# Attention with bias on one core: k and q of pair 2 ahead of V of pair 0, and a wait for the sixth load ahead in the prologue

## Chip, core and metric

The kernel runs on one core of a Trainium2 chip. The metric is device time in microseconds of one execution; the kernel before was run three times. The core's engines work side by side and meet through semaphores: TensorE (PE: matrix products and transposes, with weight loads listed apart as PEld), VectorE (DVE), ScalarE (ACT), GpSimd (POOL), and SyncE (SP), which only issues DMA transfers. PE, ACT and DVE each execute their instructions in the order in which the program lists them, and so do the queues that issue transfers.

## What is computed

Four batches of eight heads, each with 1024 positions and 64 dimensions; one bias of 1024 x 1024 for all heads.

```
scores = scale * matmul(q, k.T) + bias          # scale = 1/8
attn   = exp(scores - max) / sum(exp(scores - max))
out    = matmul(attn, v)                        # f32, (4, 8, 1024, 64)
```

## The kernel before

**Tiling.** The 32 heads are taken in 16 pairs, because two heads of 64 dimensions fill the 128 partitions. A head's 1024 queries are cut into 8 chunks of 128. One unit of work, a *slot* (256 in all), is one chunk of one head: eight products of 128 x 128 write the scores of 128 queries against 1024 keys into one of three places in PSUM (`pl0` to `pl2`, line 87; the fill is at L244), an exponential on ACT reads the place and writes the tile E (L258), and later eight products of E with V give the output with the row sums beside it (L312). DVE takes the reciprocal and scales (L320, L322), and SP stores. 19 slots, listed in `PLAN`, have their exponential computed on DVE instead (L275 to L295).

**Bias once for many heads.** Scores stay in their PSUM place from one head to the next: the bias of a chunk is put in once by products (L241), and each later head adds the difference from the head before. That is why a pair has `ko` and `qo` for its odd head and `ke` and `qe` for the even one, which hold rows of this pair and of the pair ahead of it. L199 and L201 copy `ko` and `qo` out of PSUM; L210 and L212 make the doubles in `ke` and `qe`; for later pairs, and for half of `ke` from pair 2 on, SP copies by DMA (L539).

**Loads.** k, q and V arrive in f32 and are turned to bf16 by the transfer itself, which POOL issues: L145 for k, L155 for q, L165 for V, L160 for a bias chunk. k and q of a pair are transposed on PE (L191) into PSUM tiles `px` that share two PSUM tiles with the output banks `po`; V is copied by DVE into `vall` (L493), which the products of L312 read. There are three landing tiles for V (`VL`), five each for k and q (`LANDS`). A transfer issued on POOL has one of eight semaphores in turn and waits for the transfer that had it before, so at most eight of POOL's loads are out at a time.

**What sets the order.** The first instructions stand by hand (lines 337 to 392): the loads of pair 0, then bias chunks 1 and 2, k of pair 1, the first part of q of pair 1, V of pair 0, k of pair 2 and q of pair 2 on POOL. From line 394 a planner writes the rest of the program: it keeps a clock for each engine (`t_pe`, `t_act`, `t_dve`, `t_pool`, `t_sp`), asks for each possible next step when it could start by estimated costs and landing times, and records the step that is first. `raw_at` holds the time at which k or q of a pair is taken to have landed, `vland_at` that of V; `t_dma` is the clock of the load queue. These are estimates that decide the order alone; on the chip semaphores decide.

`early` issues the 21 loads of the list in line 772: k3, q3, V1, k4, q4, V2, k5, q5, V3, k6, q6, V4, V5, bias 3, the rest of q0, bias 4, V6, the rest of q1, bias 5, 6 and 7. All later loads (pair 7 on) come from `load` and `next_v`. Both go through `issue`, whose third argument is a depth: where it is above 0, POOL first copies one element of the load that stands so many places back in `flight` into `tick` (L468), which can only run once that load has landed.

```
if 0 < depth <= len(flight):
    what, t = flight[-depth]
    nc.gpsimd.tensor_copy(tick[:], what)
    at = max(at, t + 100)
```

`load` and `next_v` use a depth of 2 or 3 (`LATE`); `early` uses 0.

Of the kernel before, what the change touches and what calls it, by code (L numbers as in the profile page):

```python
# [16 lines left out]
def kernel(  # L17
# [30 lines left out]
    SPLIT, EARLY = 2, 7  # L48
# [84 lines left out]
    def beside(pr, x):  # L133

        raws[pr, x, 0] = t = land.tile([P, 2, NCH, D], BF, name="qk"[x] + "16").rearrange(
            "p t c d -> p (t c d)").rearrange("p (c t d) -> p c t d", t=2, d=D)
        for y in range(2):
            nc.gpsimd.dma_start(out=t[:, :, y, :], in_=(qf, kf)[x][pr][:, y].rearrange("p (c d) -> p c d", d=D))  # L138
        return t[:1, NCH - 1, 1, D - 1:]

    def load_k(pr):
        if pr >= EARLY and 1 in BESIDE:
            return beside(pr, 1)
        lands[pr, 1, 0] = t = land.tile([P, 2, NCH, D], BF, name="k16")
        nc.gpsimd.dma_start(out=t.rearrange("p t c d -> p t (c d)"), in_=kf[pr])  # L145
        return t[:1, 1, NCH - 1, D - 1:]

    def load_q(pr, cs):
        if pr >= EARLY and 0 in BESIDE:
            return beside(pr, 0)  # L150

        t = consts.tile([P, 2, NCH - C0, D], BF, name=f"qrest{pr}") if cs.start else land.tile([P, 2, NCH, D], BF, name="q16")
        lands[pr, 0, cs.start] = t
        to = t[:, :, :cs.stop - cs.start, :]
        nc.gpsimd.dma_start(out=to.rearrange("p t c d -> p t (c d)"),  # L155
                            in_=qf[pr][:, :, cs.start * D:cs.stop * D])
        return to[:1, 1, cs.stop - cs.start - 1, D - 1:]
# [5 lines left out]
    def load_v(pr):  # L163
        lands[pr, "v"] = vland.tile([P, 2, NCH, D], BF, name="v16")
        nc.gpsimd.dma_start(out=lands[pr, "v"].rearrange("p t c d -> p t (c d)"),  # L165
                            in_=vf[pr].rearrange("p t c d -> p t (c d)"))
        return lands[pr, "v"][:1, 1, NCH - 1, D - 1:]
# [167 lines left out]
    with tc.manual_schedule():  # L335
# [17 lines left out]
            load_b(c)  # L353
        load_k(1)
        load_q(1, slice(0, C0))
        load_v(0)
        load_k(2)
        load_q(2, slice(0, NCH))
        for i in range(10):
            nc.tensor.matmul(places[2][:, 0, :], zeros[:, :P], zeros, start=True, stop=True)  # L360

# [35 lines left out]
        ISSUE, COPY = 70, 7000  # L397
        T0 = 8600.0
        bias_at = {0: T0, 1: T0, 2: 9600}
        raw_at = {(1, 1, 0): 10800, (1, 0, 0): 11500, (2, 1, 0): 14300, (2, 0, 0): 16000}  # L400
        v_at, vland_at = {}, {0: 13000}
        t_dma = 15500
        DUE = (62, 84, 100, 38, 118, 109, 123, 147, 135)
        t_pe, t_act, t_dve, t_pool = 9300.0, 9900.0, 9600.0, 9000
# [31 lines left out]
        E1, E2 = 1400, 1700  # L436
        free_lands, loads, loads_v = set(), list(range(EARLY, NP)), []
        sp_q, t_sp = [], T0
        AHEAD, SLACK = 60, 300
# [23 lines left out]
        def issue(at, cost, depth, load, pr, *a):  # L463

            nonlocal t_dma
# [4 lines that stand above are left out]
            at = pool(at, 750)  # L470
            t_dma = max(t_dma + cost, at + 2200 + cost)
            flight.append((load(pr, *a), t_dma + 200))
            return t_dma + 200

        def load(pr, t):
            raw_at[pr, 1, 0] = issue(t, 1600, LATE, load_k, pr) + SLACK
            raw_at[pr, 0, 0] = issue(t, QCOST, LATE, load_q, pr, slice(0, NCH)) + SLACK
            for p in [pr - 1] * (pr > EARLY) + [pr] * (pr + 1 == NP):
                loads_v.append(p)
            next_v(t)  # L480
# [10 lines left out]
        def move_v(pr):  # L491
            def run(t2):
                nc.vector.tensor_copy(vall[:, 2 * pr % VR:2 * pr % VR + 2, :, :D], lands[pr, "v"][:])  # L493
                v_at[pr] = t2 + 480 + L_DVE
                next_v(v_at[pr])
            dve_q.append((vland_at[pr] + VSLACK * (pr >= EARLY), 0.3, 480, run))


        def early(kind, pr):
            if kind == "k":  # L500
                raw_at[pr, 1, 0] = issue(0, E1, 0, load_k, pr) + SLACK
            elif kind == "q":
                cs = slice(0 if pr >= SPLIT else C0, NCH)
                raw_at[pr, 0, cs.start] = issue(0, E1 if pr >= SPLIT else E2, 0, load_q, pr, cs) + SLACK
            elif kind == "v":
                vland_at[pr] = issue(0, E1 if pr < 5 else E2, 0, load_v, pr)
                move_v(pr)
            else:
                bias_at[pr] = issue(0, E2, 0, load_b, pr)

        def doubles(pr, which, c0, n, t2, urgent):
            if not which and pr >= EARLY:
# [165 lines left out]
        def pool(at, cost=0):  # L678
            nonlocal t_pool
            t_pool = max(t_pool, at) + cost  # L680
            return t_pool
# [90 lines left out]
        for x in ("k3", "q3", "v1", "k4", "q4", "v2", "k5", "q5", "v3", "k6", "q6", "v4", "v5", "b3", "q0", "b4", "v6", "q1", "b5", "b6", "b7"):  # L772
            early(x[0], int(x[1]))
# [71 lines left out]
```

## Time and profile before

| | us |
|---|---|
| median of 3 runs | 234.18 (233.77 to 234.87) |
| the profiled execution | 234.37 |
| its span, first to last instruction | 232.6 |
| granted TensorE clock in it | 0.998 of full |

The profile is that of one execution. The span is what its views cover; the execution's own time is 1.8 us longer. A row of the timeline gives the start, the length, the engine, the line of the code, the operation, what it writes from what it reads, how many instructions are taken together, and in brackets how long the engine idled before and what ended that. In the list of exponentials the mean of one (1104 ns) is longer than the step from one to the next, because they overlap in the pipeline. The last number of a DMA issue row is the time from the issue to the landing.

### The profile page before, as it was taken

What the parts mean: (1) busy time and instruction counts of PE and PEld (TensorE: products, weight loads), DVE (VectorE), ACT (ScalarE), POOL (GpSimd) and SP (SyncE); (2) the same over time, 40 slices, a digit from 0 to 9 for tenths busy, and PEclk for the clock granted to TensorE, in tenths of its full rate; (3) what the DMA queues carried; (4) which work ended last, traced back from release to release, by engine and by line L of the source; (5) the groups of instructions that cost most, each with busy time, mean ns of one, the idle gap of its engine ahead of it and who ended that gap; (6) DMA issues with size and microseconds to landing.
All of it is one profiled execution on the core that took longest, in us unless ns stands there. A gap on an engine that the chain in (4) does not pass through costs nothing.

```text
span 232.6 us, 10671 instructions
## 1 busy us (share of the span) xinstructions
PE 223.1 (96%) x4671; PEld 209.8 (90%) x4671; DVE 197.4 (85%) x294; ACT 221.6 (95%) x242; POOL 61.6 (27%) x99
## 2 busy tenths in 40 slices
PE   7979999899999999999999999999999999999993
PEld 2869997899999999999999999999998999999992
DVE  3566777599988998989889789899999899999993
ACT  3799999899999999999999999999999999999994
POOL 8844440155633524445244110000000000000000
PEclk9999999999999999999999999999999999999999
DMA  6999999899999999989899865111112122112212
GB/s 205 205 205 218 222 225 216 188 108 121 152 176 141 153 183 143 135 183 194 150 241 216 188 107 130 43 37 39 42 29 57 34 53 50 58 28 74 70 37 62
DMA packets 55645, 29.75 MB, mean 128 GB/s; under 512 B 31856, under 2 KB 51952, under 8 KB 55600
## 3 DMA queue, kind: packets, MB, share of 16 engines
q0 software_dynamic: 30336, 14.06, 48.5%
q1 hardware_dynamic: 24832, 14.43, 22.5%
q8 instruction: 36, 0.59, 1.0%
q10 hardware_dynamic: 432, 0.59, 0.8%
q14 instruction: 9, 0.07, 0.1%
HBM read 29.36 MB, written 8.39 MB: 162 GB/s over the span
## 4 chain that ended last, share of the span: by engine, by line
PE 42%; ACT 30%; issue 14%; DMA 5%; DVE 4%; POOL 3%; SPq 2%; DVEq 0%; ACTq 0%; POOLq 0%
ACT E L258 30%; PE pl L244 24%; PE po L312 12%; DMA q<-in_q_dram 4%; PE px L191 4%; SPq L694 2%; PE pl L241 2%; DVE ob L322 1%; DMA out_dram<-ob 1%; DVE dy L275 1%; POOL k L145 1%; DVE df L280 1%; POOL braw L160 1%; DVE dt L290 0%; DVE de L295 0%
## 5 line engine op out<-in xcount | busy, mean ns | idle before, releaser
L258 ACT ACTIVATE E<-pl 128x1024 bf16<-128x1024 f32 (+1 forms) x238 | 218.5, 1104 | 3.5 <-PE pl L244 3.1
L312 PE MATMUL po<-vall,E 128*128 128x65 bf16 x1896 | 92.0, 194 | 1.5 <-DVE ob L322 0.8
L312 PEld LDWEIGHTS <-E 128*128 128x128 bf16 x1896 | 77.4, 98 | 2.8 <-ACT E L258 1.1
L244 PE MATMUL pl<-qo,ko 128*128 128x128 bf16 x1024 | 76.8, 219 | 0.8 <-ACT E L258 0.2
L244 PEld LDWEIGHTS <-ko 128*128 128x128 bf16 x1160 | 69.4, 98 | 3.9 <-issue 0.7
L244 PE MATMUL pl<-qe,ke 128*128 128x128 bf16 x888 | 66.3, 219 | 1.7 <-issue 0.6
L244 PEld LDWEIGHTS <-ke 128*128 128x128 bf16 x888 | 53.5, 98 | 4.6 <-issue 0.7
L275 DVE TENSOR_SCALAR dy<-pl 128x1024 int32<-128x1024 f32 x19 | 23.2, 1221 | 4.5 <-PE pl L244 3.7
L322 DVE TENSOR_TENSOR ob<-po,rs 128x448 f32<-128x448 f32 (+2 forms) x40 | 23.2, 581 | 2.7 <-DMA out_dram<-ob 0.8
L284 DVE SCALAR_TENSOR_TENSOR dt<-df 128x1024 f32<-128x1024 f32 x19 | 23.2, 1220 | 0.3
L295 DVE SCALAR_TENSOR_TENSOR de<-dy,dt 128x1024 uint16<-128x1024 int32 x19 | 23.1, 1218 | 0.1
L287 DVE SCALAR_TENSOR_TENSOR df<-dt,df 128x1024 f32<-128x1024 f32 x19 | 23.1, 1218 | 0.1
L290 DVE SCALAR_TENSOR_TENSOR dt<-df,dt 128x1024 f32<-128x1024 f32 x19 | 23.0, 1217 | 0.1
L138 POOL DMA_DIRECT2D q<-in_q_dram x18 | 16.4, 911 | 2.9 <-PE pl L244 1.6
L201 DVE TENSOR_SCALAR qo<-px,sgn 128x1024 bf16<-128x1024 bf16 (+2 forms) x18 | 12.4, 687 | 4.9 <-PE px L191 3.2
L165 POOL DMA_DIRECT2D v<-in_v_dram x16 | 11.6, 728 | 16.3 <-DVE rs L320 7.5
L199 DVE COPY ko<-px 128x1024 bf16<-128x1024 bf16 (+1 forms) x16 | 10.7, 670 | 5.5 <-PE px L191 5.3
L320 DVE RECIPROCAL rs<-po 128x7 f32<-128x7 f32 (+3 forms) x42 | 8.1, 193 | 6.7 <-PE po L312 6.3
L280 DVE TENSOR_SCALAR df<-dy 128x1024 f32<-128x1024 uint16 x19 | 13.0, 686 | 0.1
L241 PE MATMUL pl<-ident,braw 128*128 128x128 bf16 x136 | 11.5, 228 | 0.1
L145 POOL DMA_DIRECT2D k<-in_k_dram x15 | 10.6, 710 | 2.5 <-DMA k<-in_k_dram 0.9
L468 POOL COPY tick<-q 1x1 bf16<-1x1 bf16 x9 | 3.3, 365 | 28.4 <-DMA q<-in_q_dram 28.4
(54 smaller groups left out, 126.2 us busy)
## 6 DMA issues: line engine op xcount, KB each, us to landing
v<-in_v_dram POOLq DMA_DIRECT2D x16, 256.0 KB, 6.6
k<-in_k_dram POOLq DMA_DIRECT2D x15, 256.0 KB, 6.0
out_dram<-ob SPq DMA_DIRECT2D x35, 96.0 KB, 3.9
ke<-ko SPq DMA_DIRECT2D x22, 128.0 KB, 4.4
out_dram<-ob SPq DMA_DIRECT2D x40, 64.0 KB, 2.5
q<-in_q_dram POOLq DMA_DIRECT2D x18, 128.0 KB, 5.2
out_dram<-ob SPq DMA_DIRECT2D x68, 32.0 KB, 2.9
qe<-q SPq DMA_DIRECT2D x17, 128.0 KB, 5.0
```

The lines of the kernel that those rows point to most:

```text
L138: nc.gpsimd.dma_start(out=t[:, :, y, :], in_=(qf, kf)[x][pr][:, y].rearrange("p (c d) -> p c d", d=D))
L241: nc.tensor.matmul(to, braw[:, c, :].rearrange("p (kp kc) -> p kc kp", kc=NCH)[:, kc, :], ident8[:], start=i == 0, stop=False, skip_group_ ...
L244: nc.tensor.matmul(to, kk[:, kc, :], qq[:, c, :], start=False, stop=True, skip_group_check=True)
L258: nc.scalar.activation(e[:, i:i + n].rearrange("p b x -> p (b x)"), places[slots[s][0]][:, i:i + n].rearrange("p b x -> p (b x)"), ACTF.Ex ...
L275: w.tensor_scalar(t["y"][:], places[slots[s][0]].rearrange("p b x -> p (b x)"), scale * LOG2E * 65536.0, 127.0 * 65536.0, op0=ALU.mult, op ...
L280: w.tensor_scalar(t["f"][:], t["lo"], G / 65536.0, None, op0=ALU.mult)
L284: w.scalar_tensor_tensor(t["t"][:], t["f"][:], -G, t["f"][:], op0=ALU.add, op1=ALU.mult)
L287: w.scalar_tensor_tensor(t["f"][:], t["t"][:], Q, t["f"][:], op0=ALU.mult, op1=ALU.add)
L290: w.scalar_tensor_tensor(t["t"][:], t["f"][:], V, t["t"][:], op0=ALU.add, op1=ALU.mult)
L295: w.scalar_tensor_tensor(etile[s].bitcast(U16).rearrange("p c q -> p (c q)"), t["y"][:], 1.0 / 512.0, t["t"][:], op0=ALU.mult, op1=ALU.add)
L312: nc.tensor.matmul(po[:, j + i, :], etile[s][:, kc, :], vall[:, slots[s][2] % VR, kc, :], start=j + i + kc == 0, stop=kc == NCH - 1, skip_ ...
L322: nc.vector.tensor_tensor(ob[:, :n, :], po[:, :n, :D], rs[:, :n, :].to_broadcast([P, n, D]), op=ALU.mult)
```

## The change

Two edits. The first takes V of pair 0 behind k and q of pair 2 in the hand-written list, and gives the planner matching landing times. The second calls `issue` in `early` with a depth of 6 instead of 0.

```
         load_k(1)
         load_q(1, slice(0, C0))
-        load_v(0)
         load_k(2)
         load_q(2, slice(0, NCH))
+        load_v(0)
...
-        raw_at = {(1, 1, 0): 10800, (1, 0, 0): 11500, (2, 1, 0): 14300, (2, 0, 0): 16000}
-        v_at, vland_at = {}, {0: 13000}
+        raw_at = {(1, 1, 0): 10800, (1, 0, 0): 11500, (2, 1, 0): 12700, (2, 0, 0): 14300}
+        v_at, vland_at = {}, {0: 16300}
...
         def early(kind, pr):
             if kind == "k":
-                raw_at[pr, 1, 0] = issue(0, E1, 0, load_k, pr) + SLACK
+                raw_at[pr, 1, 0] = issue(0, E1, 6, load_k, pr) + SLACK
             elif kind == "q":
                 cs = slice(0 if pr >= SPLIT else C0, NCH)
-                raw_at[pr, 0, cs.start] = issue(0, E1 if pr >= SPLIT else E2, 0, load_q, pr, cs) + SLACK
+                raw_at[pr, 0, cs.start] = issue(0, E1 if pr >= SPLIT else E2, 6, load_q, pr, cs) + SLACK
             elif kind == "v":
-                vland_at[pr] = issue(0, E1 if pr < 5 else E2, 0, load_v, pr)
+                vland_at[pr] = issue(0, E1 if pr < 5 else E2, 6, load_v, pr)
                 move_v(pr)
             else:
-                bias_at[pr] = issue(0, E2, 0, load_b, pr)
+                bias_at[pr] = issue(0, E2, 6, load_b, pr)
```

The depth takes hold from the seventh of the 21 loads: k5 waits for k3, q5 for q3, and so on to bias 7, 15 copies (L468) more on POOL. What follows in the program: on PE the transposes of k2 stand ahead of fill 6 instead of behind fill 7, those of q2 ahead of fill 8 instead of behind it, and the first product with V stands behind fill 11 instead of fill 13 (fills are counted as slots, from 0); from fill 19 on, PE's order is that of before. On DVE the copy of V0 moves behind the first double of q2, and the first evacuation of an output bank moves ahead of q4's copy. ACT's and SP's order is that of before.

## The prediction

> **What bounds the kernel now.** I read the page first, then the activations by stage, then the stage with the idle time, row by row.
>
> ```profile
> span 232.6 us, 10671 instructions
> PE 223.1 (96%) x4671; PEld 209.8 (90%) x4671; DVE 197.4 (85%) x294; ACT 221.6 (95%) x242; POOL 61.6 (27%) x99
> ...
> PE 42%; ACT 30%; issue 14%; DMA 5%; DVE 4%; POOL 3%; SPq 2%; DVEq 0%; ACTq 0%; POOLq 0%
> ```
>
> PE and ACT are both nearly full and the chain of waits changes between them; DMA holds 5% of it. Which of the two decides where, the stretches of the exponentials (L258) show:
>
> ```profile
> core 0: us, ACT busy (x), PEclk, DMA share, GB/s
> 8.00:17.43 9.43, 8.45 (x10) 1.00 1.25 201
> 17.43:38.62 21.19, 21.18 (x23) 1.00 1.21 219
> 38.62:50.76 12.14, 10.75 (x13) 1.00 1.03 171
> 50.76:232.60 181.84, 178.03 (x194) 1.00 0.62 107
> ...
> L258 ACT ACTIVATE E<-pl 128x1024 bf16<-128x1024 f32 x194 | 178.2, 1112 | 0.6 <-PE pl L244 0.5
> ```
>
> From 50.76 on ACT runs 194 exponentials at 0.918 us each; most of the 3.81 us it is not busy there is the tail, since its list of groups from 50.8 on (last row) has 0.6 us of waiting. So whatever ACT gains or loses before 50.76 goes to the end one for one, if nothing later is tied to absolute time. Before 50.76 it idles 0.98 + 0.01 + 1.39 us. That is the whole purse: no reordering of early loads can win more than some 2.4 us. The early idle time, from the timelines:
>
> ```profile
> 8.99 7.93 ACT L258 ACTIVATE E<-pl 128x512 bf16<-128x512 f32 x9 [0.47 <-PE pl L244]
> 17.43 21.19 ACT L258 ACTIVATE E<-pl 128x1024 bf16<-128x1024 f32 x23 [0.51 <-PE pl L244]
> ...
> 12.14 0.62 PE L244 MATMUL pl<-qo,ko 128*128 128x128 bf16 x8
> ...
> 12.91 0.25 DVE L212 TENSOR_SCALAR qe<-qo 64x384 bf16<-64x384 bf16 x1
> ...
> 13.22 1.07 PE L244 MATMUL pl<-qe,ke 128*128 128x128 bf16 x16 [0.46 <-DVE qe L212]
> ...
> 14.22 0.64 PE L191 MATMUL px<-ident,k 128*64 128x128 bf16 x16
> 14.79 0.62 PE L244 MATMUL pl<-qe,ke 128*128 128x128 bf16 x8
> ...
> 16.21 0.64 PE L191 MATMUL px<-ident,q 128*64 128x128 bf16 x16 [0.80 <-DMA q<-in_q_dram]
> 16.78 1.07 PE L244 MATMUL pl<-qo,ko 128*128 128x128 bf16 x16
> 17.77 0.64 PE L191 MATMUL px<-ident,k 128*64 128x128 bf16 x16
> ...
> 20.37 0.42 PE L312 MATMUL po<-vall,E 128*128 128x65 bf16 x8
> ```
>
> At 16.21 PE, which runs in order, waits 0.80 us for q of pair 2 (q2) though the fills behind it, of pair 1, need nothing of q2; ACT then stands 0.51 us. The chain of waits says the same: q2's load is its longest single piece.
>
> ```profile
> 7.18 8.98 DMA q<-in_q_dram
> ```
>
> **Part 1, k2 and q2 ahead of V of pair 0 (v0).** The next rows are the issues of v0, k2 and k3 on POOL's timeline, and the same three in the list of DMA issues, one window each, with the time to landing last.
>
> ```profile
> 5.77 0.74 POOL L165 DMA_DIRECT2D v<-in_v_dram  x1
> 6.48 0.74 POOL L145 DMA_DIRECT2D k<-in_k_dram  x1
> ...
> 7.87 0.76 POOL L145 DMA_DIRECT2D k<-in_k_dram  x1
> ...
> v<-in_v_dram POOLq DMA_DIRECT2D x1, 256.0 KB, 6.6
> ...
> k<-in_k_dram POOLq DMA_DIRECT2D x1, 256.0 KB, 7.2
> ...
> k<-in_k_dram POOLq DMA_DIRECT2D x1, 256.0 KB, 9.1
> ```
>
> Landings before: v0 12.4, k2 13.7, q2 16.2, k3 17.0. Three loads of one size change places in one queue, so I let each take its place's landing: k2 12.4, q2 13.7, v0 16.2, k3 still 17.0. The program's new order on PE is: fill 5, k2's transposes, fills 6 and 7, q2's transposes, fills 8, 9, 10, k3's transposes, fill 11, the first attn-V product.
> - Fill 5 starts at 12.14 and leaves PE at about 12.6 (0.45 to 0.5 us a fill: two from 16.78 to the next block at 17.77). k2's transposes (0.57: 14.22 to 14.79) go from 12.6 to 13.2, into the 0.46 us that PE idled. Fill 6 waits for DVE's qe, which ends at 13.16: it starts at 13.2 as before. Cost 0; its cover is only 0.2 us of k2's landing, past which fill 6 slips.
> - Fills 6 and 7 to 14.2, q2's transposes to 14.8 (landed 13.7, 0.5 to spare), fill 8 at 14.8, as before. DVE meets v0's copy later, where it waits for its landing (16.2); behind it are one qe copy for pair 3 and k3's ko. The first attn-V product stood at 20.37 and moves to about 18, so v0 has over 1 us to spare. Cost 0.
> - Fill 9 stood behind q2's transposes at 16.78. Now it waits only for its PSUM place, which the exponential of fill 6 frees. ACT's nine end at 16.92 and are 0.92 apart, so that one ends near 15.1, and fill 9 is done by 15.9, a microsecond before ACT wants it. The 0.51 us gap closes.
> - Late next is k3: PE comes to it at 16.7, waits 0.3 us, and fill 11 is done at 18.0; ACT wants it at 16.92 + 2 x 0.92 = 18.76. Covered by 0.7.
>
> So ACT gains 0.51 us, and PE about 0.8 (k3's transposes stood at 17.77, now 17.0). From 17.43 to 38.62 ACT had no gap, so there it is the bound and PE's further 0.3 us goes into earlier products. In 38.62 to 50.76 its 1.39 us of idle time come from PE waits that I take to move along with the work:
>
> ```profile
> 36.90 0.45 PE L244 MATMUL pl<-qe,ke 128*128 128x128 bf16 x5 [0.58 <-issue]
> ...
> 43.55 0.69 PE L312 MATMUL po<-vall,E 128*128 128x65 bf16 x16 [0.79 <-DVE ob L322]
> ```
>
> The second is PE waiting for the evacuation of a bank that its own product had just finished. PE's order beyond the first attn-V products is that of before, block for block. Bounds for part 1: gain 0 (k3 or v0 holds PE instead) to 0.51 + 1.39 = 1.90; I take 0.51, the row with the known cause.
>
> **Part 2, the wait for the sixth load ahead.** Each of the 15 loads from k5 on gets a one-element POOL copy (L468) that waits for a landing. Behind it on POOL, until k7, stand only later copies and loads; so the price is how much later data lands. One such copy and the load it releases, a slow one, and loads k5, v5 (issued at 13.96 and 25.29) and k7:
>
> ```profile
> 44.60 0.18 POOL L468 COPY tick<-braw 1x1 bf16<-1x1 bf16 x1 [9.09 <-DMA braw<-in_bias_dram]
> 45.10 0.70 POOL L145 DMA_DIRECT2D k<-in_k_dram  x1 [0.32 <-issue]
> ...
> 59.62 1.19 POOL L468 COPY tick<-q 1x1 bf16<-1x1 bf16 x1 [3.29 <-DMA q<-in_q_dram]
> ...
> k<-in_k_dram POOLq DMA_DIRECT2D x1, 256.0 KB, 11.7
> ...
> v<-in_v_dram POOLq DMA_DIRECT2D x1, 256.0 KB, 9.4
> ...
> k<-in_k_dram POOLq DMA_DIRECT2D x1, 256.0 KB, 3.9
> ```
>
> k3 lands at 17.0 and v5, twelve loads on, at 25.29 + 9.4 = 34.7: 1.48 us a load, and the busy times by stretch, whose last two columns are DMA share and rate, show the engines full:
>
> ```profile
> core 0: us, PE busy (x) PEld busy (x) DVE busy (x) ACT busy (x) POOL busy (x), PEclk, DMA share, GB/s
> ...
> 17.43:38.62 21.19, 20.61 (x466) 18.93 (x464) 15.18 (x33) 21.18 (x23) 8.81 (x13) 1.00 1.21 219
> ```
> An empty queue lands k7 in 3.9 us, so most of k5's 11.7 is queueing. With the gate a load is issued 0.5 us after the landing six ahead, when five loads, 5 x 1.48 = 7.4 us, are still to land ahead of it; it needs 3.9. Margin 3.0 us, with a 1.19 us copy 2.0. k5's issue moves from 13.96 to about 17.5, its landing does not. Cost 0; the cover is the five queued loads. If it were gone, all of a load's landing time would be exposed (the slower rival). Below zero: a shorter queue could speed SyncE's copies, but none of their waits stands in the early idle time; no gain.
>
> The copies use POOL's and DVE's way to SBUF. The Trainium skill (SBUF — State Buffer, "SBUF: two separate sides") speaks against them: a GpSimd instruction and a DVE instruction in a two-port mode exclude each other for their whole length. The 0.18 and 1.19 us rows above would fit that, though the trace does not name the port. By the rule fifteen copies could hold DVE for 15 x 0.18 = 2.7 us, an estimate, which the 6.0 us that DVE idles in the stretch above would take in; the sum by it is the same.
>
> **Sum.** Profiled execution 234.37 us (span 232.6 and 1.8 around it): 234.37 - 0.51 + 0 = 233.86. It lies 0.19 above the median of 234.18, so against the median 233.7.
>
> **The rivals.**
> - *Slower: the queue starves.* If a load's time to landing is mostly latency that stays with six in flight, say 10.8 us (between the 9.4 and 11.7 rows), k5 lands at 17.5 + 10.8 = 28.3 and v5, which waits for k5, at 28.3 + 0.5 + 10.8 = 39.6, not 34.7. DVE runs in order and already meets V copies that wait for landings:
>
> ```profile
> 34.72 0.43 DVE L493 COPY vall<-v 128x1024 bf16<-128x1024 bf16 x1 [0.28 <-DMA v<-in_v_dram]
> ...
> 35.78 0.68 DVE L199 COPY ko<-px 128x1024 bf16<-128x1024 bf16 x1
> ...
> 37.28 0.64 PE L191 MATMUL px<-ident,q 128*64 128x128 bf16 x16
> ```
>
>   Behind v5's copy stand an evacuation and k6's ko, which free the two PSUM tiles that PE needs next for q6 at 37.28. The ko ends at 36.46, and PE comes 0.5 earlier, so a slip of v5 by 0.3 us starts to hold PE; 4.9 us hold it 4.6; ACT is fed for up to three places, 2.8, so it loses 1.8 to 4.6. Less 0.51: 235.5 to 238.3, middle 236.9; half the slip costs about nothing to 1.8. For it: nothing in the trace has only six in flight. Against it: the 3.9 us row and the full engines.
> - *No gain.* k3 slips past its 0.7 us of cover, or the 2.5 us between k2's and q2's landings belongs to the load and not to its place (q2 then lands at 14.9, and 0.7 of PE's time is lost again at 14.2). 234.0 to 234.3.
> - *More gain.* PE's further lead also shortens the two waits of 0.58 and 0.79, and ACT's 1.39 us close: 234.18 - 1.90 = 232.3. For it: ACT's gaps there are put down to PE. Against: both causes travel with PE.
>
> **How the numbers follow.** Forecast 0.57 (233.3 to 234.1), no gain 0.11, queue starves 0.20, more gain 0.12. What a measurement of this kernel can tell from no change is about 0.5%, 1.17 us: below 233.0 is faster, above 235.35 slower. Faster: 0.11 of the more-gain case and 0.02 of the forecast's edge, 0.13. Slower: 0.17 of the 0.20 (a partial slip stays inside). Same: 0.70. The range leaves out half of the more-gain case below and about 0.14 of the starving case above: 232.7 to 235.6; the likeliest case alone has 233.3 to 234.1.
>
> **What would show it.** Right: q2 lands by 14.2 and its transposes have no DMA wait; ACT runs from 8.99 to 38.1 without the 0.51 gap; k5 is issued near 17.5 and lands near 25.7, v5 near 34.7; the gaps of 38 to 51 return half a microsecond earlier. Wrong: fill 6 later than 13.5 (k2 late), PE waiting on k3 beyond 17.7, V copies on DVE waiting over 1 us, the DMA share below 1.2 between 20 and 38, or an ACT gap after 51.

## The result and the profile after

| | before | after |
|---|---|---|
| median, 22 runs each | 234.23 us | 233.44 us |
| ratio, with its 95% interval | | 0.9965 (0.9949 to 0.9981) |
| a second series of the same kernel (11 runs, 22 of before) | 234.31 | 233.19; 0.9952 (0.9929 to 0.9975) |
| the profiled execution, its span | 234.37, 232.6 | 233.77, 232.0 |

The change is worth 0.8 us (0.0035 x 234.23), 1.1 in the second series: a small gain that its interval sets apart from nothing. The forecast was 0.51.

One thing has to be known before times in the two profiles are compared. This execution began its first exponential at 8.44 us, the one of before at 7.92. Its first loads, of bias and of q and k of pair 0, landed 0.3 to 0.5 us later; the change touches none of them. PE's and ACT's times until about 17 us are therefore half a microsecond later than the working of the prediction has them.

The exponentials of the kernel after by stretch (ACT busy, number, clock, DMA share, rate), cut where its own gaps are, and the list of groups of ACT from 50.2 on:

```profile
core 0: us, ACT busy (x), PEclk, DMA share, GB/s
8.00:16.92 8.92, 8.01 (x10) 1.00 1.25 203
16.92:38.10 21.18, 21.18 (x24) 1.00 1.22 218
38.10:50.20 12.10, 11.17 (x13) 1.00 1.01 176
50.20:232.00 181.80, 177.99 (x194) 1.00 0.64 107
...
L258 ACT ACTIVATE E<-pl 128x1024 bf16<-128x1024 f32 x194 | 178.3, 1114 | 0.6 <-PE pl L244 0.5
```

The last 194 exponentials take 178.3 us with 0.6 of waiting, as before (178.2, 0.6): what was won was won ahead of 50 us and reached the end. ACT's timeline and PE's show where:

```profile
9.51 30.89 ACT L258 ACTIVATE E<-pl 128x512 bf16<-128x512 f32 x34 [0.47 <-PE pl L244]
40.69 3.77 ACT L258 ACTIVATE E<-pl 128x1024 bf16<-128x1024 f32 x4 [0.29 <-ACT E L258]
44.84 4.89 ACT L258 ACTIVATE E<-pl 128x1024 bf16<-128x1024 f32 x5 [0.39 <-PE pl L244]
...
13.20 0.64 PE L191 MATMUL px<-ident,k 128*64 128x128 bf16 x16
13.77 1.07 PE L244 MATMUL pl<-qe,ke 128*128 128x128 bf16 x16
14.77 0.64 PE L191 MATMUL px<-ident,q 128*64 128x128 bf16 x16
15.34 0.62 PE L244 MATMUL pl<-qe,ke 128*128 128x128 bf16 x8
15.79 0.61 PE L244 MATMUL pl<-qo,ko 128*128 128x128 bf16 x8
...
17.30 0.64 PE L191 MATMUL px<-ident,k 128*64 128x128 bf16 x16
```

Where ACT had three rows with two gaps (0.51 at 17.43, 0.20 at 38.83) it has one row of 34 exponentials. The transposes of k2 (13.20) and q2 (14.77) stand between the fills without a wait in brackets; the wait of 0.80 us for q2 is gone. Fill 9 starts at 15.79, a full microsecond earlier than before in spite of the later start.

The loads, in the list of DMA issues (time to landing last), one window each: k2, q2 and v0, issued at 5.79, 6.48 and 7.18, and k5, issued at 17.65.

```profile
k<-in_k_dram POOLq DMA_DIRECT2D x1, 256.0 KB, 6.8
...
q<-in_q_dram POOLq DMA_DIRECT2D x1, 256.0 KB, 7.4
...
v<-in_v_dram POOLq DMA_DIRECT2D x1, 256.0 KB, 9.5
...
k<-in_k_dram POOLq DMA_DIRECT2D x1, 256.0 KB, 8.0
```

k2 lands at 12.6, q2 at 13.9, v0 at 16.6. k5 is issued 3.7 us later than before (13.96) and lands at 25.7, at which it landed before too. The wait for the sixth load takes its time out of the load's own queueing.

### The profile page after: what moved, and what is told of

Read it like the earlier page. It is cut to its first block, busy times and chain, and to the rows that moved or that the text cites. A ratio compares the mean times of both kernels' runs of the same rounds, so it can differ in the third digit from the quotient of the medians.

```text
span 232.0 us, 10693 instructions
## 1 busy us (share of the span) xinstructions
PE 223.4 (96%) x4671; PEld 210.0 (91%) x4671; DVE 196.8 (85%) x294; ACT 221.5 (95%) x242; POOL 64.6 (28%) x114
## 4 chain that ended last, share of the span: by engine, by line
ACT 25%; PE 15%; issue 11%; DMA 6%; DVE 6%; SPq 1%; DVEq 0%; ACTq 0%
ACT E L258 25%; PE pl L244 10%; PE po L312 4%; DMA out_dram<-ob 3%; DMA qe<-q 3%; SPq L694 1%; DVE ob L322 1%; DVE dt L290 1%; DVE dy L275 1%; DVE de L295 1%; PE px L191 1%; DVE df L280 1%; DVE df L287 0%; PE pl L241 0%; DVE rs L320 0%
## 5 line engine op out<-in xcount | busy, mean ns | idle before, releaser
L322 DVE TENSOR_TENSOR ob<-po,rs 128x448 f32<-128x448 f32 (+2 forms) x40 | 23.2, 581 | 3.4 <-DVE rs L320 1.1
L201 DVE TENSOR_SCALAR qo<-px,sgn 128x1024 bf16<-128x1024 bf16 (+2 forms) x18 | 12.4, 686 | 3.4 <-PE px L191 1.7
L468 POOL COPY tick<-q 1x1 bf16<-1x1 bf16 x13 | 4.2, 321 | 26.2 <-DMA q<-in_q_dram 25.9
```

The source lines that it names most:

```text
L201: nc.vector.tensor_scalar(t["qo"][:, cs, :], px[:], sgn[:], None, op0=ALU.mult)
L322: nc.vector.tensor_tensor(ob[:, :n, :], po[:, :n, :D], rs[:, :n, :].to_broadcast([P, n, D]), op=ALU.mult)
```

## The experiments

All kernels keep the order of instructions on PE and DVE of the kernel that they start from, so that only what is named differs. Each was timed together with before, and its ratio is to before of the same series.

**The order of the loads alone** (the changed kernel, depth 0, so with its order on PE and DVE):

```
-                raw_at[pr, 1, 0] = issue(0, E1, 6, load_k, pr) + SLACK
+                raw_at[pr, 1, 0] = issue(0, E1, 0, load_k, pr) + SLACK
...
```

> The changed kernel without the wait for the sixth load (depth 0 again); PE's and DVE's order is that of the changed kernel. Theory 1 (the whole gain is that q2 lands ahead of v0 and PE no longer waits for it): as the changed kernel, ratio to before 0.996 to 0.998; ACT's 0.51 us gap ahead of fill 9 is gone; k5 is issued near 14 instead of 17.6 and lands at 25.7 all the same. Rival (the shorter queue brings the part of the gain above 0.51 us, because PE's two waits of 0.58 and 0.79 us near 36.5 and 43 shrink to 0.30 and 0.51 with it): those two waits are back at about 0.6 and 0.8, and the kernel is 0.3 to 0.5 us slower than the changed one.

Measured: 233.34 us, ratio 0.9968 (0.9949 to 0.9987). ACT's timeline and PE's:

```profile
8.95 30.86 ACT L258 ACTIVATE E<-pl 128x512 bf16<-128x512 f32 x34 [0.47 <-PE pl L244]
...
44.79 4.87 ACT L258 ACTIVATE E<-pl 128x1024 bf16<-128x1024 f32 x5 [0.92 <-PE pl L244]
...
17.05 0.64 PE L191 MATMUL px<-ident,k 128*64 128x128 bf16 x16 [0.43 <-DMA k<-in_k_dram]
```

The first edit alone brings what both bring. It holds two things, the places of the loads and the order that the planner makes of them on PE and DVE; no run has the one without the other, but two runs below move a load with PE's order kept. Late next is k3, as worked out, and its 0.43 us does not reach ACT. The rival does not hold as it was put: the wait of PE near 36.5 is gone here, without the shorter queue; the one near 43 was longer (1.05 us).

**The wait for the sixth load alone** (before, depth 6 in the four calls):

```
-                raw_at[pr, 1, 0] = issue(0, E1, 0, load_k, pr) + SLACK
+                raw_at[pr, 1, 0] = issue(0, E1, 6, load_k, pr) + SLACK
...
```

> The kernel before with the wait for the sixth load alone; PE's and DVE's order is that of before. Theory 1: no change, within 0.2 us of before; q2 lands at 16.2 as before, PE's 0.80 us wait and ACT's 0.51 us gap stand, k5 is issued near 17.5 and lands near 25.7. Rival (the shorter queue shortens PE's waits near 36.5 and 43): 0.3 to 0.5 us faster than before, with those waits at 0.3 and 0.5. Second rival (six in flight starve the queue): V5 lands after 35.5 and the kernel is slower.

Measured: 234.33, ratio 1.0015 (0.9989 to 1.004): nothing that shows. k5 is issued at 17.2 and lands at 25.6, V5 at 34.2. On PE's timeline and ACT's the waits of before are all there:

```profile
16.18 0.64 PE L191 MATMUL px<-ident,q 128*64 128x128 bf16 x16 [0.60 <-DMA q<-in_q_dram]
...
17.41 21.20 ACT L258 ACTIVATE E<-pl 128x1024 bf16<-128x1024 f32 x23 [0.39 <-PE pl L244]
38.96 1.94 ACT L258 ACTIVATE E<-pl 128x1024 bf16<-128x1024 f32 x2 [0.35 <-PE pl L244]
```

**k2 alone ahead of v0:**

```
-        load_v(0)
         load_k(2)
+        load_v(0)
         load_q(2, slice(0, NCH))
```

> The kernel before with k2 alone ahead of v0, q2 still behind it, no wait for the sixth load; PE's and DVE's order is that of before. Theory 1 (q2's landing is what PE waits for): q2 still lands near 16.2, PE's wait for it stays at 0.6 to 0.9 us, ACT's gap at about 0.5, time within 0.2 us of before. Rival (it is k2's earlier landing, or v0's place in the queue, that brings the gain): 0.3 us or more faster than before.

Measured: 234.04, ratio 0.9991 (0.9978 to 1.0004). q2 landed at 16.0; PE waited 0.64 us for it, and ACT's gap was 0.41. It is q2's place that counts, not k2's.

**q2 one place later still**, behind k3 (in `early` the load of k3 is left out, since it has been issued):

```
         load_k(2)
+        k3 = load_k(3)
         load_q(2, slice(0, NCH))
```

> The kernel before with q2 one place later still, behind k3; no wait for the sixth load; order of PE and DVE as before. Theory 1 (ACT's gap is q2's landing less the 15.65 us at which it would just be in time, 16.16 - 0.51): q2 lands near 17.0, PE waits about 1.6 us for it instead of 0.8, ACT's gap ahead of fill 9 is about 1.35 instead of 0.51, and the kernel is 0.6 to 0.9 us slower than before. Rival (PE's lead over ACT or the later bounds swallow a delay of this size, so the gap that closed was not what the time came from): within 0.3 us of before.

Measured: 235.16, ratio 1.0035 (1.0021 to 1.005), so 0.8 us slower. The same two views:

```profile
17.10 0.64 PE L191 MATMUL px<-ident,q 128*64 128x128 bf16 x16 [1.57 <-DMA q<-in_q_dram]
...
18.33 21.20 ACT L258 ACTIVATE E<-pl 128x1024 bf16<-128x1024 f32 x23 [1.31 <-PE pl L244]
```

q2 landed 0.9 us later, PE waited 0.77 more, ACT 0.80 more, and the run time grew by 0.8. This is the mechanism with its sign turned, and the strongest evidence for it: the landing of q2 goes through to the end of the kernel.

**The wait for the third, fourth and fifth load ahead.** The planner's clock is left out of these three, so that the order stays:

```
-            if 0 < depth <= len(flight):
-                what, t = flight[-depth]
+            if depth == 6 and len(flight) >= 3:
+                nc.gpsimd.tensor_copy(tick[:], flight[-3][0])
+            elif 0 < depth < 6:
+                what, t = flight[-depth]
```

> The changed kernel with each early load from k4 on waiting for the third load ahead instead of the sixth; the planner's clock is left out of it, so that PE's and DVE's order is that of the changed kernel. Theory 1 (full engines at 1.48 us a load; a load needs 3.9 us from issue to landing and 0.5 for the copy, 4.4 in all, so three in flight give 1.47 us a load at best): just at the edge; V5 lands at most 1 us later than 34.8, and the time is within 0.5 us of the changed kernel. Rival (a load needs more than that in a busy queue, say the 8 us that it takes with six in flight): 8/3 = 2.7 us a load, V5 lands after 45, DVE and PE stand behind it, and the kernel is 5 us or more slower.

> The changed kernel with each early load from q4 on waiting for the fourth load ahead, order as in the changed kernel. Theory 1 as mended by the run with three (a load needs 4.4 to 6.1 us from issue to landing with three in flight, mean about 5.1, and 0.55 for the copy, so some 5.6 in all): four in flight give 5.6/4 = 1.4 us a load, just under the 1.48 of the full engines; V5 lands by 35.5, and the time is within 0.3 us of the changed kernel. Rival (the landing time stays at the 8 us seen with six in flight): 2.1 us a load, V5 lands after 39, 3 us or more slower than the changed kernel.

> The changed kernel with each early load waiting for the fifth load ahead, order as in the changed kernel. Asked: how much room the sixth had. Theory 2 (with fewer in flight the engines idle more and more: V5 landed at 34.8 with six, 36.6 with four, 39.3 with three): V5 lands between 34.9 and 35.7, DMA share from 17.4 to 38.6 between 1.15 and 1.22, and the kernel is 0.1 to 0.5 us slower than the changed one. Rival (the edge is sharp and lies between four and five): V5 by 34.9, no difference to the changed kernel.

| waits for | in flight | V5 lands | DMA share, GB/s, 17.43 to 38.62 | time | ratio (interval) |
|---|---|---|---|---|---|
| nothing (order alone) | 8 | 35.0 | 1.22, 219 | 233.34 | 0.9968 (0.9949 to 0.9987) |
| sixth (second series) | 6 | 34.6 | 1.21, 220 | 233.19 | 0.9952 (0.9929 to 0.9975) |
| fifth | 5 | 34.9 | 1.21, 222 | 233.21 | 0.9952 (0.9928 to 0.9976) |
| fourth | 4 | 36.6 | 1.15, 187 | 234.37 | 0.9999 (0.998 to 1.0018) |
| third | 3 | 39.3 | 1.04, 169 | 238.83 | 1.0203 (1.0182 to 1.0224) |

In all three the theory was off. Three in flight was not the edge but well past it; four, which should have cost at most 0.3 us, cost 0.8 to 1.1; five, which should have cost a little, cost nothing, as the rival named for that run had it. So the edge lies between four and five. With three in flight, DVE, PE and ACT in their timelines:

```profile
31.74 0.43 DVE L495 COPY vall<-v 128x1024 bf16<-128x1024 bf16 x1 [3.20 <-DMA v<-in_v_dram]
32.08 0.68 DVE L199 COPY ko<-px 128x1024 bf16<-128x1024 bf16 x1
...
32.82 0.64 PE L191 MATMUL px<-ident,q 128*64 128x128 bf16 x16 [2.03 <-DVE ko L199]
38.94 0.64 PE L191 MATMUL px<-ident,k 128*64 128x128 bf16 x16 [1.34 <-DVE ob L322]
...
34.37 4.69 ACT L258 ACTIVATE E<-pl 128x1024 bf16<-128x1024 f32 x5 [2.25 <-PE pl L244]
40.23 3.89 ACT L258 ACTIVATE E<-pl 128x1024 bf16<-128x1024 f32 x4 [1.18 <-PE pl L244]
...
50.88 2.88 ACT L258 ACTIVATE E<-pl 128x1024 bf16<-128x1024 f32 x3 [1.69 <-PE pl L244]
```

Read from the top, this is the path of the slower rival: DVE stands 3.20 us before a V copy whose load has not landed; the copy of `ko` behind it frees the PSUM tile that PE needs for the next transposes; PE stands 2.03 us, and ACT 2.25. The three gaps sum to 5.1 us, near the 5.4 that separate this kernel from the changed one (238.83 - 233.44).

**A third output tile,** with the wait for the sixth load and without it. The room for it comes from landing the rest of q1 in a tile of the exponential on DVE.

```
-    op = ctx.enter_context(tc.tile_pool(name="op", bufs=2))
+    op = ctx.enter_context(tc.tile_pool(name="op", bufs=3))
...
+        if cs.start and pr == 1:
+            t = dp.tile([P, S], F32, name="df").bitcast(BF)[:, :2 * (NCH - C0) * D].rearrange("p (t c d) -> p t c d", t=2, d=D)
...
```

> The changed kernel with three output tiles instead of two (the room comes from landing the rest of q1 in a tile of the exponential on DVE); order as in the changed kernel. Asked: whether PE's wait near 43 (0.5 to 1.05 us in the runs so far, in one of them behind a scaling that waited 1.2 us for a store to land) comes from stores. Theory: it does only in executions in which a store is late; the wait stays at about 0.5, and the time is within 0.3 us of the changed kernel. Rival (stores set it as a rule): PE's wait near 43 falls below 0.3, ACT's gap near 45 below 0.2, and the kernel is 0.3 us or more faster than the changed one.

> The changed kernel with three output tiles and without the wait for the sixth load. Theory (order alone brings the gain, the wait and the third tile neither cost nor bring anything that can be measured): as the changed kernel, ratio to before 0.995 to 0.998. Rival (with eight in flight a third output tile pays, because stores then land late, as in the run with the order alone in which a scaling waited 1.2 us for one): 0.3 us or more faster than the order alone.

Measured: 233.25, ratio 0.9958 (0.9943 to 0.9974) with the wait, 232.94, ratio 0.9936 (0.9911 to 0.9961) without. PE's wait near 43 stayed (0.51 and 0.66 us), so stores do not set it as a rule; what does is taken up below. The second was expected at 0.995 to 0.998 and came out lower, 0.4 us below the order alone as its rival had it. But its interval overlaps those of the order alone and of the changed kernel, and it was not timed in one series with the order alone: whether the third tile brings anything is not settled.

**The changed kernel once more:**

> The changed kernel once more, on the chip of the two others. Theory 1: ratio to before 0.996 to 0.998; in the profile no gap of ACT between 9.6 and 38, no wait of PE for q2, and PE's waits near 36.5 and 43 anywhere between 0 and 1.05 us, as in the runs so far, with ACT's gap near 45 following the second of them.

Its time is in the tables above; the ratio, 0.9952, lies just below the range that was expected. ACT's timeline has one row from 8.99 to 43.6; the gap of 0.29 at 40.69 is gone too.

```profile
8.99 34.64 ACT L258 ACTIVATE E<-pl 128x512 bf16<-128x512 f32 x38 [0.47 <-PE pl L244]
44.10 4.87 ACT L258 ACTIVATE E<-pl 128x1024 bf16<-128x1024 f32 x5 [0.47 <-PE pl L244]
```

## Why the prediction was right, and where it was not

**The bound.** That ACT's idle time ahead of 50 us decides, one for one, held: q2 0.9 us later, ACT's gap 0.80 longer, the kernel 0.8 slower.

**Part 1, the landings.** Each load took its place's landing. Forecast k2 12.4, q2 13.7, v0 16.2; the second series, which starts like the profile of before, has 12.2, 13.4 and 16.2. The long step ahead of the third (2.5 us before) does not belong to one load: q2, v0 or k3 met it, whichever stood third, and in the kernel with a third tile and no wait it came one place later (v0 at 15.0, k3 at 17.0). One 16 KB transfer of the queue that the page lists as "instruction" runs at 14.1 to 15.0 in the profile of before, and one at nearly that time in the others; whether it is the cause is not shown.

**Part 1, PE's steps.** Fill 6, q2, fill 8 and fill 9 came as worked out, with no wait for k2 or q2. k3 held PE by 0.14 to 0.55 us in the seven other profiles with q2 early, which all start like that of before (forecast 0.3), without reaching ACT. Two of the signs named for a wrong forecast came and meant nothing. Fill 6 started at 13.77, later than 13.5, but with the late start of that profile; in the second series it started at 13.25. And DVE waited 1.10 and 1.08 us ahead of the V copies at 20.23 and 28.26, with no gap of ACT behind them.

**Part 1, the size.** The gap of 0.51 us closed; the change measured 0.8 and 1.1. The term that was mis-sized is the one of 38 to 51 us: I took ACT's waits there "to move along with the work", and let PE's further lead of 0.3 us go "into earlier products". They did not move along. From the second exponential to the end of the last, the three profiles with q2 behind v0 (before, the wait alone, k2 alone) have 220.17, 220.21 and 220.04 us; the six with q2 early and enough loads in flight have 219.06, 219.46, 219.51, 218.98, 218.67 and 219.28, a mean of 219.16. That is 0.98 less, 0.47 more than the gap of before. ACT's gaps ahead of 50 us show where. In the mean the gap ahead of fill 9 fell from 0.44 us to nothing, the one near 39 from 0.30 to nothing, the one near 41 from 0.29 to 0.14 and the one near 45 from 0.56 to 0.47. The last three stand in the profile of before as

```profile
38.83 1.94 ACT L258 ACTIVATE E<-pl 128x1024 bf16<-128x1024 f32 x2 [0.20 <-PE pl L244]
41.05 3.77 ACT L258 ACTIVATE E<-pl 128x1024 bf16<-128x1024 f32 x4 [0.29 <-ACT E L258]
45.48 4.87 ACT L258 ACTIVATE E<-pl 128x1024 bf16<-128x1024 f32 x5 [0.66 <-PE pl L244]
```

The one near 39 goes with one matmul, the fourth of fill 31, at which PE waited 0.58 us "on issue" before:

```
profile              16 KB instruction      PE's wait,    matmul    ACT's gap
                     transfer, us           us            starts    near 39, us
before               34.50 to 35.43         0.58          36.90     0.20
the wait alone       34.59 to 35.52         0.62          37.03     0.35
k2 alone             34.55 to 35.54         0.66          36.96     0.35
q2 later             35.58 to 36.48         0.62          37.95     0.35
the change           34.15 to 35.16         0.30          36.53     none
the change again     33.03 to 33.92         none          35.70     none
the order alone      33.53 to 34.47         none          35.95     none
fifth load           32.81 to 33.70         none          35.72     none
```

Wherever PE waited, it went on 1.4 to 1.5 us after the end of the transfer; where it did not wait, the matmul started 1.5 to 2.0 us after it, and 1.4 in the two kernels with a third tile. With q2 early, PE came to this place sooner and the transfer sooner still: in the last three rows PE began fill 30 0.2 to 0.5 us ahead of before, the transfer ended 1.0 to 1.7 us ahead, and PE did not wait. What starts a transfer the profile does not tell. So the lead that I had spent on products came with the end of a second gap of 0.20 to 0.35 us. This reading rests on the order of times in these profiles; no run moved the instruction transfer alone. The Trainium skill (Runtime: NRT & Kernel Launch, "Instruction fetch mechanics") describes engines that refill their instructions in blocks of 16 KiB over a DMA queue of their own while they execute, and calls the cost of a block's edge mostly hidden. The size agrees with these transfers; here, with the DMA engines full, up to 0.66 us was not hidden at this matmul, and the measurement decides.

The gap near 45 follows PE's wait near 43, and there the prediction misread its row. I took PE to wait for DVE's scaling (L322), as the bracket has it. But in the kernel with the order alone PE goes on at 42.86, half a microsecond before the scaling ends at 43.36:

```profile
42.80 0.56 DVE L322 TENSOR_TENSOR ob<-po,rs 128x384 f32<-128x384 f32 x1 [1.20 <-DMA out_dram<-ob]
...
42.86 0.69 PE L312 MATMUL po<-vall,E 128*128 128x65 bf16 x16 [1.05 <-issue]
```

In the profile of before the scaling ended at 43.14, and PE went on only at 43.55. The place is again one of the instructions: the matmul stands 256 of PE's products and weight loads behind the one of fill 31, and 9,342 of them in 36 transfers of 16 KB come to some 260 a transfer.

```
profile              16 KB instruction      PE's wait,    matmul    scaling    ACT's gap
                     transfer, us           us            starts    ends       near 45, us
before               41.12 to 42.05         0.79          43.55     43.14      0.66
the wait alone       41.30 to 42.25         0.79          43.68     43.27      0.65
k2 alone             40.90 to 41.78         0.50          43.32     43.20      0.38
q2 later             42.15 to 43.09         0.79          44.60     44.19      0.65
the change           40.69 to 41.63         0.51          42.91     42.77      0.39
the change again     39.81 to 40.82         0.62          42.16     41.92      0.47
the order alone      40.41 to 41.34         1.05          42.86     43.36      0.92
fifth load           39.39 to 40.39         0.22          41.89     42.05      0.08
third tile           39.76 to 40.71         0.51          42.17     42.04      0.39
third tile, no wait  40.13 to 41.05         0.66          42.59     42.31      0.54
```

In every row PE goes on 1.3 to 1.5 us after the end of the transfer, and ACT's gap is PE's wait less 0.12 to 0.15. Why the transfer comes earlier or later against PE's work stays open, and so does the gap near 41, which the profile puts down to ACT itself. Such waits can come back: in three of the six profiles with q2 early PE waits 0.48 to 0.90 us "on issue" between 119 and 126 us, where ACT lost up to 0.39.

**Part 2, cost 0.** Right: k5 was forecast to be issued near 17.5 and to land near 25.7, and did (17.65, 25.7); the wait alone changed nothing (1.0015). The margin was not right. I took 3.9 us, an empty queue's time, for what a load needs, and got room for three loads; in a queue of three a load takes 4.4 to 6.1, and four in flight already lose. The cover that I named holds at six, with one load to spare instead of three: that this depth cost nothing was in part luck. The copies themselves took 0.18 to 0.40 us in the stretch of the loads, and DVE was busy 14.65 of 21.19 us there (15.18 before). By the rule of the Trainium skill that I set against the change (SBUF — State Buffer, "SBUF: two separate sides") they could have held it 2.7 us, an estimate; no such cost shows.

**The rivals.** The starving queue was the right path for the wrong depth. Its price (1.8 to 4.6 us for a slip of V5 by 4.9) was low: with a slip of 4.5, ACT's three gaps sum to 5.1, because the first V copy that waits, ahead of k5's `ko`, already stops PE, and ACT's gap behind it (2.25) was no shorter than PE's wait (2.03): the three places that feed ACT did not cover it. *No gain* fell with q2's landing at 13.9. *More gain* named the right place, PE's lead in 38 to 51, and took too much of it: about half a microsecond of 1.39.

## What to carry to other kernels

On an engine that works in order, a transfer's price is that of the first instruction that stands behind it and doesn't need it; look in the profile for a wait on DMA just ahead of work of another stage, and move that load up by the place in the queue that it lacks, before anything else. The cap on loads in flight cost nothing here as long as the DMA share stayed where it was (1.21 or more) and cost time at 1.15, so read the share, and not an empty queue's landing time, to choose it. A lead on an engine that is not the bound can still pay where that engine has waits that need not move along with its work. And the releaser in brackets is inferred: compare its end with the start of what waited before you build on it.

## What the runs showed of the hardware

- A load of 256 KB (bf16 in SBUF) needed five in flight here to keep the DMA engines full: 222 GB/s with five, 220 with six, 187 with four, 169 with three, from 17.43 to 38.62 us. A load's own landing time grew with the number: 3.9 us in a queue that had all but run empty, 4.4 to 6.1 with three, about 8 with six, 9 to 12 with eight. Why three or four leave the engines idle was not isolated.
- PE can wait where, by the order of times, its own instructions are late: 0.30 to 0.66 us at one matmul in five profiles and 0.22 to 1.05 at the one 256 products and weight loads on, in ten. It went on 1.3 to 1.5 us after the end of a 16 KB transfer of the instruction queue, which itself took 0.9 to 1.0 us among full DMA engines.
